# Mixing stage of a hybrid mLSTM and attention layer: gates ahead of the convolutions, splits in halves, reciprocal roots in nine steps, values of two head groups in 512 columns

## The chip, the cores and the metric

The kernel runs on one core of a Trainium2 chip. The metric is the time of one execution on the device in microseconds (us). PE is TensorE (matrix products), with PEld its weight loads, DVE is VectorE, ACT is ScalarE, POOL is GpSimd and SP is SyncE, which issues the DMAs. Each engine works through its own list of instructions in order, and waits at an instruction until its inputs are there and its output buffer is free.

## The reference

One layer acts on 512 tokens of 1024 columns, in float32. A conditioning vector `c` gives nine vectors of shift, scale and gate (`mod`). Then:

```python
u = rms_norm(x, ffn1_norm_g) * (1 + sc1) + sh1
x = x + 0.5 * g1 * swiglu(u, ffn1_w_in, ffn1_w_out)          # FFN1

u = rms_norm(x, mix_norm_g) * (1 + sc2) + sh2
z = u @ w_mix + b_mix                                        # mixing
q_m, k_m, v_m, o_m, i_m, f_m, q_f, k_f, v_f, f_f, g_a, g_b = split(z)
qk_m = silu(causal_conv([q_m, k_m], conv_w, conv_b))         # width 4
h_m = mlstm_chunkwise(q_m, k_m, v_m, i_m, f_m)               # 4 heads, 128 / 256
y_a = sigmoid(o_m) * rms_norm(h_m, mlstm_norm_g)
y_b = forgetting_attention(q_f, k_f, v_f, f_f, ...)          # 16 heads of 64
merged = sigmoid(g_a) * (y_a @ w_branch_a) + sigmoid(g_b) * (y_b @ w_branch_b)
x = x + g2 * (merged @ w_out)

u = rms_norm(x, ffn2_norm_g) * (1 + sc3) + sh3
x = x + 0.5 * g3 * swiglu(u, ffn2_w_in, ffn2_w_out)          # FFN2
```

`rms_norm` divides each row by the root of its mean square plus 1e-6. The gates of both mixers (i_m, f_m with 4 columns each, f_f with 16) go through log-sigmoid and cumulative sums over the tokens.

## The kernel before, in words

**Products.** Every float32 product is made of three products of shorter floats: each operand is split into a high part (`wh`, `uh`) and the rest (`wl`, `ul`), and `mm3` (L124 to L128) adds high by high (L126), high by low (L127) and low by high (L128) into one PSUM bank; which of the two operands is called weight or input depends on the caller. Which operand is held and which streams differs: a product streams 128 to 512 columns. A weight tile comes by DMA into a buffer `raw` (three of them, L91), ACT copies it to `wh` (L101) and DVE subtracts to get `wl` (L103); of `wh` and of `wl` there are four buffers each. Such a tile holds 1024 columns in each of 128 partitions, the gates' first two 840. PSUM has four banks named `g` and four named `t`.

**Order.** A scheduler orders the instructions of each engine from the order in which the program makes them and from the buffers; in some places the program pins its own order (`self.pin`), among them the function `end` (from L1315), which passes from FFN1 to the mixing stage.

**Roots.** `rsqrt` (L136 to L154) is made of DVE instructions on few columns: two for the first guess from the bits of the number, eight for a polynomial that corrects it. `xnorm` (L241) makes the mean square of two token blocks in two steps, calls `rsqrt`, and multiplies x (L253 on DVE, and a half on ACT) to `xn`; `chain` at the start of the kernel does the same. `mlstm_h` (each head) and `fox_qkv` (each group of four heads) call `rsqrt` as well, on 4 and 32 columns.

**From FFN1 to the mixing stage.** The 512 tokens are normalised in two halves. `xn` is transposed on PE (L295), and `u_part` (L270 to L280) makes `uh` and `ul` from it for each of eight blocks k of 128 columns. In `end`, the residual updates of x (`onto`, L600) and the squares of x for the second half (`x_sq`, L228) are interleaved with the first half's u parts and with the splits of the first four weight tiles of `w_mix`, m = 0 to 3 (`hi` makes `wh` and returns the subtraction for `wl`, L1328). `first(0)` and `first(1)` (L1380 to L1390) run the products of these four tiles with the first and with the second half of the tokens: lines L1387, L1388 and L1390, six products of 256 columns for each k and pair of m. Both halves go over k = 0 to 3 for m = 0, 1, then for m = 2, 3, then k = 4 to 7 the same way. Between `first(0)` and `first(1)` stand the second half's root, transposes and u parts.

**Then** (L1416 to L1425) come the convolutions of m = 0 to 3 (`qk_conv`: `cz` on ACT L917, four steps of `cy` on DVE L919 and L921, silu and high part on ACT, low part on DVE L926), then `gates` (L850), then m = 4 to 7 with a product and a convolution each. `gates` streams 280 columns: 256 columns of v_f (the values of head group 0, kept in DRAM as `v0` for later) and the gates' 24. Their weights come in three tiles (3, 3 and 2 blocks k), each of four DMA pieces. The results fill the four `t` banks; DVE adds biases (L861 and L862 into `gz`, L863 for v0), PE transposes `gz` (L880), and ACT and DVE make logs and scans. `columns()` runs after m = 7.

**Attention.** For each group g of four heads, `fox_qkv` (L1039) makes the queries and keys in one product of 512 columns (biases added into `tk`, L1047), the root over their squares (`rsqrt`), and then, for g = 1 to 3, the values in a product of 256 columns (two weight tiles of 4 blocks k). `donev` adds the bias (`vg`, L1073), ACT takes the high part and DVE the low part (L1078) into a tile `vm`, of which three exist. The call for group g + 1 is used as filling between the heads of group g, in pieces, followed by tiles of the merging gates (`with_gates(..., n)`).

Of the kernel before, what the change touches and what calls it, by code (L numbers as in the profile page):

```python
# [20 lines left out]
P = 128  # L21
# [9 lines left out]
RSQ = (0.2740822732448578, 0.31394892930984497, 0.37500056624412537, 0.4999983012676239, 1.0)  # L31
# [15 lines left out]
class Layer:  # L47
# [88 lines left out]
    def rsqrt(self, v, n, pin=lambda i: i):  # L136

        nc, sp = self.nc, self.sp
        y = sp.tile([P, n], F32, name=self.nm("rq"), tag=f"rq{n}", bufs=4)
        t = sp.tile([P, n], F32, name=self.nm("rt"), tag=f"rt{n}", bufs=2)  # L140
        d = sp.tile([P, n], F32, name=self.nm("rd"), tag=f"rd{n}", bufs=2)
        V = nc.vector
        pin(V.tensor_scalar(y.bitcast(I32), v.bitcast(I32), 1, None, op0=ALU.logical_shift_right))
        pin(V.tensor_scalar(y.bitcast(I32), y.bitcast(I32), -1, 0x5F3759DF, op0=MUL, op1=ADD))

        pin(V.tensor_tensor(t, y, y, op=MUL))
        pin(V.tensor_tensor(t, t, v, op=MUL))
# [5 lines left out]
        pin(V.scalar_tensor_tensor(y, t, RSQ[4], y, op0=ADD, op1=MUL))  # L153
        return y  # L154
# [86 lines left out]
    def xnorm(self, hf, pool):  # L241

        nc, sp = self.nc, self.sp
        v = sp.tile([P, 2], F32, name=self.nm("v"), tag="v", bufs=2)
        s2 = self.ss[:, 2 * hf:2 * hf + 2, :]
        self.pin(nc.vector.tensor_scalar(v, s2[:, :, 0], 1.0 / D, EPS, op0=MUL, op1=ADD))
        self.pin(nc.vector.scalar_tensor_tensor(v, s2[:, :, 1], 1.0 / D, v, op0=MUL, op1=ADD))
        r = self.rsqrt(v, 2, self.pin)
        xn = []
        for i in range(2):  # L250
            x = self.x[2 * hf + i]
            d = self.xn_tiles(pool)
            self.pin(nc.vector.tensor_scalar(d[0], x[0], r[:, i:i + 1], None, op0=MUL))  # L253
# [439 lines left out]
    def start(self, st, tp):  # L693
# [16 lines left out]
        def chain(hf):  # L710
            v = sp.tile([P, 2], F32, name=self.nm("v"), tag="v", bufs=2)
            s2 = self.ss[:, 2 * hf:2 * hf + 2, :]
            pin(nc.vector.tensor_scalar(v, s2[:, :, 0], 1.0 / D, EPS, op0=MUL, op1=ADD))
            pin(nc.vector.scalar_tensor_tensor(v, s2[:, :, 1], 1.0 / D, v, op0=MUL, op1=ADD))
            return self.rsqrt(v, 2, pin)
# [323 lines left out]
    def fox_qkv(self, g, ip):  # L1039
# [28 lines left out]
        bv = self.bias_bcast([(VF + o, 256)], ip) if g else None  # L1068
        vt = ip.tile([P, NT, 4, P], F32R, name=self.nm("fvt"), tag="vm", bufs=3)
        def donev(tb, ps):  # L1070
            f = ip.tile([P, 256], F32, name=self.nm("vg"), tag="t2", bufs=3)
# [5 lines left out]
            nc.scalar.activation(vt[:, tb, :, 0:64], f4, AF.Copy)  # L1077
            nc.vector.tensor_tensor(vt[:, tb, :, 64:P], f4, vt[:, tb, :, 0:64], op=SUB)  # L1078
        def mkv(ch):
            def make():  # L1080
                sh = [P, 4, 256]
                r = self.raw(sh, [(lambda t: t, w[ch * 512:(ch + 1) * 512, VF + o:VF + o + 256]
                                   .rearrange("(k p) n -> p k n", p=P))])
                wh, wl = self.split(r, sh)
                return wh, wl, 4 * ch, 4
            return make
        self.fx[g] = (tok, vt)
# [186 lines left out]
    def run(self):  # L1274
# [10 lines left out]
        with tc.tile_pool(name="f1t", bufs=1) as tp:  # L1285
# [5 lines left out]
            with tc.tile_pool(name="f1h", bufs=1) as hp:  # L1291
# [23 lines left out]
                def end(close, scaled, onto):  # L1315
# [110 lines left out]
        with tc.tile_pool(name="att", bufs=1) as ip:  # L1426
# [152 lines left out]
```

## Time and profile before

| | us |
|---|---|
| time, median of 3 runs (lowest to highest) | 1333.39 (1333.33 to 1336.34) |
| the profiled execution: its own time | 1333.93 |
| the profiled execution: span of the trace | 1332.2 |
| DVE `wl` by L103, 250 instructions: busy, one | 293.4, 1.175 |
| ACT `wh` by L101, 250 instructions: busy, one | 253.8, 1.018 |

The profile shows one execution. A row of the timeline gives the start and the duration in us, the engine, the line of the kernel, the operation, the output and the inputs, their size, how many equal instructions follow each other (`x4`: the duration is then from the first one's start to the last one's end), and in brackets how long the engine was idle before it and what ended that. In a row of waits stand the waiting engine, tile and line, then the engine, tile and line waited for, then the sum in us, the number and the longest. In a row of groups stand the count, the busy time, the mean of one in ns, and the idle time before. Products on PE overlap: the time from one start to the next is shorter than the duration of one.

### The profile page before, as it was taken

How to read it: one execution, taken by the hardware profiler on the slowest of the kernel's cores; microseconds unless marked ns; L12 is line 12 of the kernel's file. 1: busy time of each engine (PE TensorE's matmuls, PEld its weight loads, DVE VectorE, ACT ScalarE, POOL GpSimd, SP SyncE). 2: the span in 40 equal slices, each digit the busy share in tenths (PEclk: the TensorE clock that was granted, in tenths of full speed). 3: DMA queues.
4: the chain of work that ended last, by engine and by line, in shares of the span. 5: the costliest groups of instructions: out<-in, count | busy, mean ns of one | idle time of the engine just before them, and what ended most of it. 6: DMA issues, size and time to landing. Idle time of an engine off the chain costs nothing.

```text
span 1332.2 us, 18008 instructions
## 1 busy us (share of the span) xinstructions
PE 1311.0 (98%) x6428; PEld 1098.2 (82%) x6428; DVE 966.3 (73%) x1776; ACT 625.0 (47%) x1038; POOL 42.4 (3%) x65
## 2 busy tenths in 40 slices
PE   7999999999999999999999999999999999999998
PEld 6788888878788888888888788778788888888886
DVE  7877777477788687887877778777477656635777
ACT  5533323365476655566666666334253223223742
POOL 1000000000010101000000000003010000000000
PEclk9999999999999999999999999999999999999999
DMA  9999978365835334534252636777529877534574
GB/s 291 276 321 312 317 269 284 113 182 182 280 112 144 108 101 133 159 101 117 65 155 52 181 97 190 217 248 234 163 71 334 282 248 265 201 105 134 172 267 149
DMA packets 205514, 254.21 MB, mean 191 GB/s; under 512 B 15008, under 2 KB 148800, under 8 KB 205424
## 3 DMA queue, kind: packets, MB, share of 16 engines
q1 hardware_dynamic: 205040, 252.98, 60.6%
q8 instruction: 51, 0.84, 0.3%
q14 instruction: 39, 0.32, 0.1%
q0 software_dynamic: 320, 0.06, 0.0%
q10 hardware_dynamic: 64, 0.02, 0.0%
HBM read 217.28 MB, written 35.72 MB: 190 GB/s over the span
## 4 chain that ended last, share of the span: by engine, by line
PE 85%; DVE 7%; DMA 3%; ACT 3%; issue 1%; POOL 0%; ACTq 0%; SPq 0%; DVEq 0%; POOLq 0%
PE g L128 22%; PE g L127 22%; PE g L126 22%; PE t L127 3%; PE t L128 3%; PE t L126 3%; PE g L826 2%; DVE wl L103 2%; PE t L1200 1%; PE t L1170 1%; DMA raw<-in_ffn_w_out_dram 1%; ACT wh L101 1%; PE t L1141 1%; PE t L826 1%; PE t L1142 1%
## 5 line engine op out<-in xcount | busy, mean ns | idle before, releaser
L101 ACT ACTIVATE wh<-raw 128x1024 fp32r<-128x1024 f32 (+2 forms) x250 | 253.8, 1018 | 379.2 <-PE g L127 115.0
L103 DVE TENSOR_TENSOR wl<-raw,wh 128x1024 fp32r<-128x1024 f32 (+2 forms) x250 | 293.4, 1175 | 186.9 <-ACT wh L101 155.6
L127 PE MATMUL g<-ul,wh 128*128 128x512 f32 (+1 forms) x912 | 348.1, 383 | 0.6 <-DVE ul L267 0.3
L126 PE MATMUL g<-uh,wh 128*128 128x512 f32 (+1 forms) x912 | 348.2, 384 | 0.2 <-ACT wh L101 0.2
L128 PE MATMUL g<-uh,wl 128*128 128x512 f32 (+1 forms) x912 | 347.8, 382 | 0.0
L127 PEld LDWEIGHTS g<-ul,wh 128*128 128x128 f32 x912 | 171.3, 188 | 34.0 <-POOL ul L267 1.1
L128 PEld LDWEIGHTS g<-uh,wl 128*128 128x128 f32 x912 | 171.3, 188 | 33.3
L126 PEld LDWEIGHTS g<-uh,wh 128*128 128x128 f32 x912 | 170.8, 188 | 33.0 <-issue 0.6
L126 PE MATMUL g<-wh,uh 128*128 128x512 f32 (+1 forms) x288 | 103.0, 358 | 0.0
L128 PE MATMUL g<-wh,ul 128*128 128x512 f32 (+1 forms) x288 | 102.2, 355 | 0.0
L127 PE MATMUL g<-wl,uh 128*128 128x512 f32 (+1 forms) x288 | 102.0, 354 | 0.0
L325 DVE SCALAR_TENSOR_TENSOR acc<-raw,ccol,acc 128x512 f32<-128x512 f32 (+1 forms) x70 | 66.7, 973 | 30.6 <-DMA raw<-in_w_ada_dram 30.4
L127 PE MATMUL t<-wl,A 128*128 128x512 f32 x176 | 69.2, 393 | 1.1 <-DVE wl L103 1.1
L126 PE MATMUL t<-wh,A 128*128 128x512 f32 x176 | 69.3, 394 | 0.0
L126 PEld LDWEIGHTS g<-wh,uh 128*128 128x128 f32 x288 | 54.3, 189 | 7.7 <-DVE tk L1047 0.5
L128 PEld LDWEIGHTS g<-wh,ul 128*128 128x128 f32 x288 | 54.3, 188 | 7.6
L127 PEld LDWEIGHTS g<-wl,uh 128*128 128x128 f32 x288 | 54.3, 189 | 7.3
L128 PE MATMUL g<-yh,wl 128*128 128x512 f32 x128 | 50.5, 394 | 1.3 <-DVE wl L103 1.3
L127 PE MATMUL g<-yl,wh 128*128 128x512 f32 x128 | 50.2, 393 | 0.0
L126 PE MATMUL g<-yh,wh 128*128 128x512 f32 x128 | 49.9, 390 | 0.0
L455 ACT ACTIVATE A<-E 128x768 fp32r<-128x768 f32 x22 | 18.6, 846 | 55.1 <-DVE E L454 51.0
L1152 ACT ACTIVATE S<-S,mn 128x128 f32<-128x128 f32 (+1 forms) x64 | 35.6, 557 | 17.9 <-DVE mn L1144 9.3
(347 smaller groups left out, 2192.3 us busy)
## 6 DMA issues: line engine op xcount, KB each, us to landing
raw<-in_ffn_w_in_dram SPq DMA_DIRECT2D x82, 512.0 KB
raw<-in_w_ada_dram SPq DMA_DIRECT2D x56, 512.0 KB
raw<-in_w_mix_dram SPq DMA_DIRECT2D x46, 512.0 KB
sa<-in_ffn_w_out_dram SPq DMA_DIRECT2D x22, 512.0 KB
sb<-in_ffn_w_out_dram SPq DMA_DIRECT2D x44, 256.0 KB
ws<-sa SPq DMA_DIRECT2D x22, 512.0 KB
ws<-sb SPq DMA_DIRECT2D x44, 256.0 KB
raw<-ws SPq DMA_DIRECT2D x44, 256.0 KB
```

The lines of the kernel that those rows point to most:

```text
L101: nc.scalar.activation(hi, src, AF.Copy)
L103: self.last_lo = nc.vector.tensor_tensor(lo, src, hi, op=SUB)
L126: pin(mm(ps, lh, rh, start=start, stop=False))
L127: pin(mm(ps, lh, rl, start=False, stop=False))
L128: self.last_mm = pin(mm(ps, ll, rh, start=False, stop=stop))
L325: nc.vector.scalar_tensor_tensor(a, r[:, s], c, a, op0=MUL, op1=ADD)
L455: nc.scalar.activation(A1[:, 0:3, :], E[:, 0:3, :], AF.Copy)
L826: pin(nc.tensor.matmul(acc_ps[b], (wl if p == 1 else wh)[:, b % 2, s], self.ul[k] if p == 2 else self.uh[k], start=k == 0 and p == 0, stop ...
L1141: nc.tensor.matmul(ps[:, :w], q[:, s], k[:, :w], start=True, stop=False)
L1142: nc.tensor.matmul(ps[:, :w], q[:, s], kl[:, :w], start=False, stop=True)
L1152: nc.scalar.activation(S[:, ws], S[:, ws], AF.Exp, scale=-1.0, bias=m, accum_out=sm[:, qb:qb + 1])
L1170: tr = lambda b, c, qb, kb: nc.tensor.transpose(b[:, c:c + P], S[:, P_OFF[qb] + kb * P:P_OFF[qb] + (kb + 1) * P], self.ident)
```

## The change

- `run`: `gates()` is called before `qk_conv` of m = 0 to 3 instead of behind them.
- `end`: the `wl` subtractions of m = 2 and 3 (`lo2`, `lo3`) are done in halves (blocks 0 to 3 and 4 to 7) at later places; `onto(2, 0, ...)` moves behind the u parts 6 and 7. `first(1)` goes over all eight k for m = 0, 1 and then for m = 2, 3.
- `rsqrt` has eight DVE instructions instead of ten (one for the first guess, seven for a polynomial in two quadratic factors), and the mean square in `xnorm` and `chain` one instead of two.
- `fox_qkv`: the call for group 2 makes the values of groups 2 and 3 in one product of 512 columns (four weight tiles of two blocks k), the call for group 3 makes none. The numbers of gate tiles behind the calls go from 2, 4, 4 to 2, 2, 6.

In the built program this takes 96 matmuls of 6400 from PE, 36 instructions of 1778 from DVE and one DMA from SP; ACT and POOL keep their number.

```diff
-    def rsqrt(self, v, n, pin=lambda i: i):
+    def rsqrt(self, v, n, pin=lambda i: i, gain=1.0):
...
-        t = sp.tile([P, n], F32, name=self.nm("rt"), tag=f"rt{n}", bufs=2)
+        t, q = [sp.tile([P, n], F32, name=self.nm("rt"), tag=f"rt{n}", bufs=2) for _ in range(2)]
...
-        pin(V.tensor_scalar(y.bitcast(I32), v.bitcast(I32), 1, None, op0=ALU.logical_shift_right))
-        pin(V.tensor_scalar(y.bitcast(I32), y.bitcast(I32), -1, 0x5F3759DF, op0=MUL, op1=ADD))
+        s = (gain * RSQ_LEAD) ** 0.25
+        (a0, b0), (a1, b1) = [(a * s, b * s * s) for a, b in RSQ_QUADS]
+        pin(V.tensor_scalar(y.bitcast(I32), v.bitcast(I32), -0.5, 0x5F3759DF, op0=MUL, op1=ADD))
         pin(V.tensor_tensor(t, y, y, op=MUL))
-        pin(V.tensor_tensor(t, t, v, op=MUL))
-        pin(V.tensor_scalar(d, t, -1.0, 1.0, op0=MUL, op1=ADD))
-        pin(V.tensor_scalar(t, d, RSQ[0], RSQ[1], op0=MUL, op1=ADD))
-        pin(V.tensor_tensor(t, t, d, op=MUL))
-        pin(V.scalar_tensor_tensor(t, t, RSQ[2], d, op0=ADD, op1=MUL))
-        pin(V.scalar_tensor_tensor(t, t, RSQ[3], d, op0=ADD, op1=MUL))
-        pin(V.scalar_tensor_tensor(y, t, RSQ[4], y, op0=ADD, op1=MUL))
+        pin(V.scalar_tensor_tensor(d, t, -s, v, op0=MUL, op1=MUL))
+        pin(V.tensor_scalar(d, d, s, None, op0=ADD))
+        pin(V.scalar_tensor_tensor(t, d, a0, d, op0=ADD, op1=MUL))
+        pin(V.scalar_tensor_tensor(q, d, a1, d, op0=ADD, op1=MUL))
+        pin(V.scalar_tensor_tensor(y, t, b0, y, op0=ADD, op1=MUL))
+        pin(V.scalar_tensor_tensor(y, q, b1, y, op0=ADD, op1=MUL))
...
@@ xnorm, and the same in chain
-        self.pin(nc.vector.tensor_scalar(v, s2[:, :, 0], 1.0 / D, EPS, op0=MUL, op1=ADD))
-        self.pin(nc.vector.scalar_tensor_tensor(v, s2[:, :, 1], 1.0 / D, v, op0=MUL, op1=ADD))
-        r = self.rsqrt(v, 2, self.pin)
+        self.pin(nc.vector.scalar_tensor_tensor(v, s2[:, :, 0], D * EPS, s2[:, :, 1], op0=ADD, op1=ADD))
+        r = self.rsqrt(v, 2, self.pin, D ** 0.5)
...
@@ fox_qkv
+        if g == 3:
+            self.fx[g] = tok, self.fx[g]
+            return
+        gs = ((0,), (1,), (2, 3))[g]
+        n = len(gs) * 256
...
-                nc.vector.tensor_tensor(f, ps[:, :256], bv[:, :256], op=ADD)
+                nc.vector.tensor_tensor(f, ps[:, :n], bv[:, :n], op=ADD)
...
-            f4 = f.rearrange("p (h d) -> p h d", h=4)
-            nc.scalar.activation(vt[:, tb, :, 0:64], f4, AF.Copy)
-            nc.vector.tensor_tensor(vt[:, tb, :, 64:P], f4, vt[:, tb, :, 0:64], op=SUB)
+            for i, vt in enumerate(vts):
+                f4 = f[:, i * 256:(i + 1) * 256].rearrange("p (h d) -> p h d", h=4)
+                nc.scalar.activation(vt[:, tb, :, 0:64], f4, AF.Copy)
+                nc.vector.tensor_tensor(vt[:, tb, :, 64:P], f4, vt[:, tb, :, 0:64], op=SUB)
...
-                sh = [P, 4, 256]
+                k = 8 // (2 * len(gs))
+                sh = [P, k, n]
...
-            yield from self.u_gemm_tokens([mkv(c) for c in range(2)], 256, donev)
+            yield from self.u_gemm_tokens([mkv(c) for c in range(2 * len(gs))], n, donev)
...
@@ end
                     part(2, 3)
-                    lo2()
                     u[2]()
                     u[3]()
+                    lo2(0, 4)
                     w1 = scaled(W[1], 0)
-                    lo3()
+                    lo3(0, 4)
                     part(4, 5)
                     u[4]()
                     u[5]()
                     onto(2, 1, tx[0, 1])
-                    onto(2, 0, tx[0, 0])
+                    lo2(4, NK)
+                    lo3(4, NK)
                     part(6, 7)
                     u[6]()
                     u[7]()
+                    onto(2, 0, tx[0, 0])
...
-                        for ks in (range(4), range(4, NK)):
+                        for ks in ((range(NK),) if h else (range(4), range(4, NK))):
                             for ms in ((0, 1), (2, 3)):
...
@@ run
+            columns = self.gates(mp, yp)
             for m in range(4):
                 self.qk_conv(m, self.pp[m], yp, mp)
-            columns = self.gates(mp, yp)
...
-                    fill = with_gates(self.fox_qkv(g + 1, ip), 4 if g else 2) if g < 3 else (s for m in range(NK) for s in self.y_a(m, yp, ip))
+                    fill = with_gates(self.fox_qkv(g + 1, ip), (2, 2, 6)[g]) if g < 3 else (s for m in range(NK) for s in self.y_a(m, yp, ip))
```

More of the change, by code (lines that the diff above doesn't have):

```diff
@@ L30 @@
 BIG = 1e30
-RSQ = (0.2740822732448578, 0.31394892930984497, 0.37500056624412537, 0.4999983012676239, 1.0)
+RSQ_LEAD = 0.2740822732448578
+RSQ_QUADS = ((-1.0965162378196741, 1.8032570710297795), (2.2419713071789813, 2.0233052502305482))
 QM, KM, VM, OM, IG, FG, QF, KF, VF, FFG, GA, GB = (
@@ L1067, in fox_qkv @@
             nc.vector.tensor_tensor(t3, t3, r[:, tb * 8:(tb + 1) * 8].unsqueeze(2).to_broadcast([P, 8, 64]), op=MUL)
-        bv = self.bias_bcast([(VF + o, 256)], ip) if g else None
-        vt = ip.tile([P, NT, 4, P], F32R, name=self.nm("fvt"), tag="vm", bufs=3)
+        if g == 3:
[3 more added lines that the diff above has]
+        n = len(gs) * 256
+        bv = self.bias_bcast([(VF + o, n)], ip) if g else None
+        vts = [ip.tile([P, NT, 4, P], F32R, name=self.nm("fvt"), tag="vm", bufs=3) for _ in gs]
@@ L1070, in donev @@
         def donev(tb, ps):
-            f = ip.tile([P, 256], F32, name=self.nm("vg"), tag="t2", bufs=3)
+            f = ip.tile([P, n], F32, name=self.nm("vg"), tag="t2", bufs=3)
             if g:
-                nc.vector.tensor_tensor(f, ps[:, :256], bv[:, :256], op=ADD)
+                nc.vector.tensor_tensor(f, ps[:, :n], bv[:, :n], op=ADD)
             else:
                 nc.sync.dma_start(f, self.v0_d[tb])
-            f4 = f.rearrange("p (h d) -> p h d", h=4)
-            nc.scalar.activation(vt[:, tb, :, 0:64], f4, AF.Copy)
@@ L1083, in make @@
                                    .rearrange("(k p) n -> p k n", p=P))])
                 wh, wl = self.split(r, sh)
-                return wh, wl, 4 * ch, 4
+                return wh, wl, k * ch, k
             return make
-        self.fx[g] = (tok, vt)
+        self.fx[g] = (tok, vts[0])
+        if len(gs) > 1:
+            self.fx[3] = vts[1]
         if g:
-            yield from self.u_gemm_tokens([mkv(c) for c in range(2)], 256, donev)
+            yield from self.u_gemm_tokens([mkv(c) for c in range(2 * len(gs))], n, donev)
```

7 lines of the change are left out of this document (3 added, 4 removed).

## The prediction

> **What bounds the kernel now.** I read the page's head and chain first, then the busy time of each engine in five stretches, then what PE waits for around the edit, and then the time rows there.
>
> ```profile
> span 1332.2 us, 18008 instructions
> PE 1311.0 (98%) x6428; PEld 1098.2 (82%) x6428; DVE 966.3 (73%) x1776; ACT 625.0 (47%) x1038; POOL 42.4 (3%) x65
> ...
> PE 85%; DVE 7%; DMA 3%; ACT 3%; issue 1%; POOL 0%; ACTq 0%; SPq 0%; DVEq 0%; POOLq 0%
> ```
>
> PE (the matrix engine) is busy for 98% of the span, and 85% of the chain that ends last lies on it. So an edit counts only by what it takes off PE's own list, or by a gap of PE that it closes or opens. Work removed from DVE (73%) or ACT is worth nothing by itself.
>
> ```profile
> 60.00:270.00 210.00, 210.00 (x927) 173.11 (x926) 149.40 (x192) 67.39 (x77) 0.00 (x0) 1.00 0.82 272
> 375.00:425.00 50.00, 46.15 (x344) 43.76 (x343) 41.31 (x83) 33.10 (x61) 5.62 (x12) 1.00 0.41 105
> ...
> 560.00:770.00 210.00, 208.74 (x1186) 180.21 (x1184) 163.97 (x437) 131.13 (x269) 0.00 (x0) 1.00 0.39 112
> 950.00:1000.00 50.00, 49.01 (x301) 42.35 (x301) 32.98 (x72) 23.69 (x44) 5.95 (x8) 1.00 0.32 98
> ```
>
> The columns are the stretch, its length, then PE, PEld, DVE, ACT and POOL busy, the granted clock, the DMA share and GB/s. PE has no gap in the long weight stages (210.00 of 210.00), and the clock is 1.00 everywhere, so no term below comes from the clock. In the transition from FFN1 to the mixing stage (375 to 425 us) PE is idle for 3.85 us; in the attention stage for 1.26 us of 210; at the start of FFN2 for 0.99 us of 50. These three are the places where this edit can win time. PE's waits in the first of them:
>
> ```profile
> PE t L127 <- DVE wl L103: 2.8, 1, 2.8
> PE t L295 <- DVE xn L253: 0.7, 1, 0.7
> PE g L1388 <- DVE wl L1328: 0.2, 1, 0.2
> ```
>
> **The change part by part.**
>
> *1. Gates ahead of the convolutions (transition).* The 2.8 us wait is the gates' own product, waiting for the low half of its first weight tile:
>
> ```profile
> 404.82 0.68 PE L126 MATMUL t<-wh,uh 128*128 128x280 f32 x4
> 408.26 0.40 PE L127 MATMUL t<-wl,uh 128*128 128x280 f32 x1 [2.76 <-DVE wl L103]
> ...
> 420.41 0.48 PE L126 MATMUL g<-uh,wh 128*128 128x512 f32 x1
> ```
> ```profile
> 402.82 0.55 DVE L919 TENSOR_SCALAR cy<-cz,colA 128x512 f32<-128x512 f32 x1 [4.15 <-ACT cz L917]
> 404.53 2.73 DVE L921 SCALAR_TENSOR_TENSOR cy<-cz,colA,cy 128x512 f32<-128x512 f32 x4
> 407.18 1.02 DVE L103 TENSOR_TENSOR wl<-raw,wh 128x840 fp32r<-128x840 f32 x1
> ...
> 420.09 0.16 DVE L861 TENSOR_TENSOR gz<-t,bb 128x8 f32<-128x8 f32 x1
> 420.63 2.35 DVE L103 TENSOR_TENSOR wl<-raw,wh 128x1024 fp32r<-128x1024 f32 x2
> ```
> ```profile
> 402.02 1.27 ACT L917 ACTIVATE cz<-g,colA 128x512 f32<-128x512 f32 x2 [4.66 <-PE g L1390]
> 403.18 2.40 ACT L101 ACTIVATE wh<-raw 128x840 fp32r<-128x840 f32 x3
> ...
> 412.48 1.07 ACT L101 ACTIVATE wh<-raw 128x1024 fp32r<-128x1024 f32 x1 [1.86 <-DMA raw<-in_w_mix_dram]
> ```
>
> The bracket is the idle time of the engine and what ended it: DVE stood idle for 4.15 us and ACT for 4.66 us. Then ACT took two convolutions' inputs before the gates' wh, and DVE took two convolutions' steps (402.82 to about 407.2) before the gates' wl. PE ran the four high products that need no wl, 0.13 us apart, so the next was due at 404.82 + 4 x 0.13 = 405.34; it began at 408.26. **2.9 us** are lost. Why were the engines idle instead of splitting? All four wh and wl buffers held the weights of m = 0 to 3 until the second half's products were done. Now first(1) does m = 0, 1 over all eight k and then m = 2, 3, so two pairs of buffers come free halfway. Where that is comes out of these rows:
>
> ```profile
> 387.87 0.17 DVE L246 TENSOR_SCALAR v<-ss 128x2 f32<-128x2 f32 x1 [0.79 <-ACT rs L228]
> 390.06 0.16 DVE L153 SCALAR_TENSOR_TENSOR rq<-rt,rq 128x2 f32<-128x2 f32 x1
> 390.26 0.88 DVE L253 TENSOR_SCALAR xn<-x,rq 128x512 f32<-128x512 f32 x2
> ```
> ```profile
> 390.89 2.16 PE L295 MATMUL t<-ident,xn 128*128 128x128 f32 x16 [0.72 <-DVE xn L253]
> 392.81 0.36 PE L1387 MATMUL g<-uh,wh 128*128 128x256 f32 x1
> ```
> ```profile
> 642.50 0.28 PE L127 MATMUL g<-wl,uh 128*128 128x256 f32 x1
> ...
> 645.02 0.28 PE L127 MATMUL g<-wl,uh 128*128 128x256 f32 x1
> ...
> 571.00 0.39 PE L126 MATMUL g<-wh,uh 128*128 128x512 f32 x1
> ...
> 575.08 0.39 PE L126 MATMUL g<-wh,uh 128*128 128x512 f32 x1
> ```
>
> A product of 256 columns follows the one before by 0.120 us (642.50 to 645.02 is 21 of them), so 8 k x 6 products take 5.8 us: from 392.81 to 398.6, the last result at about 399.0, and 398.2 with the 0.8 us of part 2. ACT, free by then, needs 2.40/3 = 0.8 us for the first wh (399.0) and DVE 1.0 us for its wl (400.0). PE wants that wl at 404.5, so the 2.9 us go with 4 us to spare.
>
> What is late next? The transposes of gz stand right behind the gates' last product on PE, and wait for DVE's gz adds. Before, DVE ran from 402.82 to the third of these adds (420.09) in 17.3 us without a break; in the new order the stretch from the first gate split to that add loses one low half and one conv step (0.7 each) and gets one more split (2.35/2): about 17.1 us, so from 399.0 to 416.1. PE comes there at 404.5 + (420.27 - 408.26) = 416.5 (it was at the first two of those transposes at 420.27). The slack is 0.4 us in a list of 17; I book a loss of 0.1 (0 to 0.5).
>
> ```profile
> 387.54 1.81 SPq L934 DMA_DIRECT2D bb<-in_b_mix_dram  x4
> ...
> 389.39 29.66 SPq L91 DMA_DIRECT2D raw<-in_w_mix_dram  x8
> ```
>
> Queues: on SP the gates' bias pieces are issued at 387.5 to 389.3 and the last of their weight pieces right behind, ten microseconds ahead of their split; the change lets them stay there. The raw buffer of m = 4 comes free with the first gate split: before, that was 408.2, and its wh began at 412.48, 4.3 us later; now about 400 and 404.3, and it is wanted after the gates (416.5). GpSimd only gets the memsets of cz later. The convolutions, now behind the gates, are read after m = 7 alone. Term: -2.9 + 0.1 = **-2.8 us** (-2.9 to -2.3).
>
> *2. Split in halves, nine steps instead of twelve (transition).* The second half's root, from 387.87 to 390.06 and 0.16 more (ended by xn at 390.26), is 12 steps of 0.2 us (2.39/12); it becomes 9: 0.6 us earlier, and the transposes behind it (390.89) with it, since PE waits there (0.72). The x updates ahead of it end perhaps 0.2 us earlier, since u parts no longer stand behind a split of 1024 columns. I take -0.8 (-0.4 to -1.2). The wait for L1388 (0.2) goes as well, but only lengthens the wait for xn behind it: nothing. Term: **-0.8 us**.
>
> *3. Values of two groups in 512 columns.* 192 products of 256 columns become 96 of 512:
>
> ```profile
> L126 PE MATMUL g<-wh,uh 128*128 128x256 f32 x96 | 27.6, 288 | 0.0
> ```
>
> These 96 of L126, with as many of L127 and L128, are the three groups' values; two groups' share is 192. A product of 512 columns takes 4.08/18 = 0.2267 us (571.00 to 575.08), two of 256 take 0.240. 96 x 0.0133 = **-1.3 us**. The busy mean of 288 ns is no price here, since products overlap; the spacing is. The Trainium skill's page "TensorE: Matmul & The Clock Gate", section "Back-to-back issue gap", puts the spacing of an isolated product at N/2.4 + 2.5 ns. By that a pair saves 2.5 ns, an estimate of 0.24 us for 96, and the total would come out 1.0 us higher; the trace's spacing at 256 columns is 120 ns where the formula gives 109, so the trace has a larger fixed part, and I go by the trace.
>
> *4. Attention stage, other effects.* The stage has 1.26 us of gaps in all. Roots of eight steps instead of ten shorten a latency there, and the gate tiles that fill PE's list are dealt out differently (2, 2, 6 instead of 2, 4, 4).
>
> ```profile
> L1047 DVE TENSOR_TENSOR tk<-g,bb 128x512 f32<-128x512 f32 x16 | 10.4, 684 | 9.7 <-PE t L1113 9.6
> ...
> L1078 DVE TENSOR_TENSOR fvt<-vg,fvt 128x256 fp32r<-128x256 f32 x16 | 6.5, 414 | 0.3 <-ACT fvt L1077 0.3
> ```
>
> A finished bank of 512 value columns now costs DVE 0.68 + 2 x 0.41 = 1.5 us, so 6.0 us for four banks in one burst; what follows on PE needs the first of them at once but the second only after a gate tile of 24 products, 24 x 0.2267 = 5.4 us. If DVE has other work in between it costs the difference and a little more, 0.8 us; if nearly all gaps closed it would give 1.0. I take **-0.2 us** (+0.8 to -1.0). The same root stands once in the mLSTM heads where PE waits:
>
> ```profile
> 545.35 0.35 PE L126 MATMUL t<-vm,Wh 128*128 128x258 f32 x1 [0.48 <-DVE hn L1027]
> ```
>
> Two steps of 0.2 fewer ahead of it: **-0.3 us** (0 to -0.5).
>
> *5. Start of FFN2.* The same xnorm stands there, and PE has gaps of 0.99 us:
>
> ```profile
> 970.52 0.68 PE L295 MATMUL t<-ident,xn 128*128 128x128 f32 x4
> ...
> 991.58 0.38 PE L127 MATMUL g<-ul,wh 128*128 128x256 f32 x1 [0.31 <-DVE ul L267]
> ```
>
> With 0.6 us less of root, the transposes move ahead of products that cover the steps behind them. I take two thirds of the gaps: **-0.7 us** (0 to -1.0).
>
> *6. Start of the kernel.* The roots get shorter there too, but PE waits for ACT:
>
> ```profile
> 16.73 1.19 PE L826 MATMUL g<-uh,wh 128*128 128x512 f32 x4 [1.19 <-ACT uh L773]
> ```
>
> ACT's columns uh come out of the modulation as well as out of the root, and I count the root as hidden behind the modulation: **0** (+0.2 to -0.4, a third of that wait).
>
> Sum: -2.8 - 0.8 - 1.3 - 0.2 - 0.3 - 0.7 = **-6.1 us**. The profiled execution took 1333.93 us (its span 1332.2 and 1.7 around it), 0.54 above the median 1333.39. 1333.39 - 6.1 = **1327.3 us**.
>
> **The rivals.**
>
> *A, the forecast:* 1327.3 us.
>
> *B, the wait moves to the gates' gz adds.* The wl wait goes, but DVE's 17.1 us ahead of the gz transposes then set the end: a first gate split that starts d later than 399.4 costs d. With a start at 400.9, as if ACT had two u parts of the second half and a tile of wh still in front of it, 1.5 us are lost there, and with the 0.8 of part 2 gone as well (DVE late in its whole list) the time is 1327.3 + 1.5 + 0.8 = **1329.6 us**. For it: the slack is 0.4 us, and DVE is busy for 41.31 of these 50 us. Against it: DVE had 4.15 us of idle time just there.
>
> *C, slower: the buffers do not come free halfway.* A split waits for the last reader of the buffer that it takes over. If the gates' splits start only when all of first(1) is done (404.0), wh is there at 404.8 and wl at 405.8, which holds PE for 1.3 us; the gz adds then end at 404.8 + 17.1 = 421.9 and PE arrives at 405.8 + 12.0 = 417.8, held 4.1 us more. 5.4 us are lost instead of 2.9 + 0.8: the stage is 1.7 us longer than before. The point from which it decides is a first gate split at 399.4 + 3.7 = 403.1. With the small terms at nothing and the values' 1.3 it gives 1333.39 + 1.7 - 1.3 = **1333.8 us**, slower than before; with the attention burst's 0.8, 1334.6. For it: the trace of before shows all of these buffers freed together, at the end. Against it: the new order frees m = 0 and 1, the oldest two, first.
>
> *D, the values' merge gives only what the page's formula gives* (part 3): 1327.3 + 1.0 = **1328.3 us**. The trace's 120 ns against 109 speaks against that rule. It lies inside A's own ends.
>
> **How the numbers follow.** A 0.75 with D in it, B 0.16, C 0.06, and 0.03 for a cost that I did not see. A's own ends: all gains at their upper bounds, -2.9 - 1.2 - 1.3 - 1.0 - 0.5 - 1.0 - 0.4 = -8.3 (1325.1); terms 4 to 6 missing and half of part 2, -4.5 (1328.9). The range reaches over B to **1324.8 to 1330.8**. A measurement of this kernel can tell 0.3% (4.0 us) from no change: faster means below 1329.4. A's lower part and a third of B fall there: **faster 0.77, same 0.19, slower 0.04**. (C at 1334 is within 0.3%; only with more late splits does it pass 1337.4.)
>
> **What would show it.** In the changed kernel's trace: the wait of the first L127 with 280 columns gone, its wl split starting at about 399 to 400 and before the first convolution step; the transposes of gz without a wait over 0.5 us; xn's transposes at about 390.1 instead of 390.89; the group of 256 columns of `wh,uh` down from 96 to 32 and the 512s up by 32 on each line, spacing 0.227; FFN2's gaps (950 to 1000) below 0.6 us. It would be wrong if the first gate split started after 403, if a new wait on gz over 1 us appeared, or if the attention stage's PE gaps grew beyond 2 us.

## The result, and the profile after

The changed kernel takes 1328.04 us (median of 5 runs, 1325.84 to 1328.99), the kernel before 1334.26 (median of 5, 1333.33 to 1336.34): a ratio of 0.9949 with a 95% interval of 0.9935 to 0.9963, so 6.8 us less by the ratio. A repeat on another chip gave 0.9948 (0.9934 to 0.9962). One execution of a later kernel (the one that makes a subtraction four times over) ran in a slower state, at 1868.43 us and a mean clock of 0.655, and is left out of its median and count. The profiled execution took 1328.68 us, its span 1326.9. Lines of `split`, `mm3` and what follows stand one or two numbers later than before (`wl` L103 is L104, the three products L126 to L128 are L127 to L129).

The page's head and chain, then the busy time in two of the stretches shown of before:

```profile
span 1326.9 us, 17767 instructions
PE 1308.3 (99%) x6332; PEld 1091.9 (82%) x6332; DVE 959.9 (72%) x1740; ACT 622.6 (47%) x1038; POOL 43.8 (3%) x65
...
PE 91%; DVE 4%; ACT 2%; DMA 2%; issue 1%; POOL 0%; SPq 0%; ACTq 0%; DVEq 0%; POOLq 0%
```
```profile
375.00:425.00 50.00, 49.43 (x366) 46.86 (x364) 42.22 (x85) 34.84 (x64) 5.90 (x13) 1.00 0.46 122
560.00:770.00 210.00, 208.79 (x1096) 175.29 (x1095) 167.03 (x435) 132.04 (x275) 0.00 (x0) 1.00 0.38 111
```

PE's idle time in the transition fell from 3.85 to 0.57 us; in the attention stage it is where it was (1.21 against 1.26). Of PE's waits between 370 and 425 us one row is left:

```profile
PE t L295 <- DVE xn L253: 0.4, 1, 0.4
```

The time rows of the transition, PE, then DVE, then ACT:

```profile
391.67 2.17 PE L295 MATMUL t<-ident,xn 128*128 128x128 f32 x16 [0.36 <-DVE xn L253]
...
405.60 0.29 PE L127 MATMUL t<-wh,uh 128*128 128x280 f32 x1
405.73 0.29 PE L128 MATMUL t<-wl,uh 128*128 128x280 f32 x1
...
418.09 0.77 PE L879 MATMUL t<-ident,gz 128*96 128x128 f32 x3
418.62 0.48 PE L127 MATMUL g<-uh,wh 128*128 128x512 f32 x1
```
```profile
400.86 1.98 DVE L104 TENSOR_TENSOR wl<-raw,wh 128x840 fp32r<-128x840 f32 x2 [1.48 <-ACT wh L102]
402.75 1.00 DVE L918 TENSOR_SCALAR cy<-cz,colA 128x512 f32<-128x512 f32 x2
...
418.26 0.15 DVE L860 TENSOR_TENSOR gz<-t,bb 128x8 f32<-128x8 f32 x1
```
```profile
399.92 1.70 ACT L102 ACTIVATE wh<-raw 128x840 fp32r<-128x840 f32 x2 [1.79 <-PE g L1400]
401.53 1.25 ACT L916 ACTIVATE cz<-g,colA 128x512 f32<-128x512 f32 x2
```

The gates' products with wh and with wl now follow each other 0.13 us apart: the 2.8 us wait is gone. Both low halves run at 400.86, ahead of the first convolution step, four microseconds before PE asks. Three transposes of gz span 0.77 us from 418.09; in the run with the gates moved alone, below, three take 0.49. 0.24 us is lost on the third gz add (418.26), 17.4 us behind the start of the wl; 17.1 were forecast. The two traces' times can't be compared one by one (PE's first instruction comes at 6.27 us instead of 4.81), but the wl starts 9.2 us behind xn's transposes; 8.9 were forecast (390.1 to 399.0).

The share of time in which PE is busy hides short delays, since products overlap. So for the terms I added up, over all neighbours on PE, the time from start to start less the usual spacing of that size (0.227 us for 512 columns, 0.129 for 280, 0.120 for 256, 0.109 for the transposes). The lost time by stretch of the two profiled executions:

| stretch, us | before | after | difference | predicted |
|---|---|---|---|---|
| 0 to 67 | 7.7 | 7.4 | -0.3 | 0 |
| 67 to 366, FFN1 | 3.3 | 4.0 | +0.7 | 0 |
| 366 to 400, roots and halves | 2.35 | 1.31 | -1.0 | -0.8 |
| 400 to 433, gates | 3.10 | 0.43 | -2.7 | -2.8 |
| 433 to 560, with the mLSTM | 1.0 | 0.9 | -0.1 | -0.3 |
| 560 to 770, attention | 5.66 | 5.67 | 0 | -0.2 |
| 770 to 933, branches | 3.4 | 1.5 | -1.9 | 0 |
| 933 to 1000, FFN2's start | 4.13 | 3.65 | -0.5 | -0.7 |
| from 1000 | 0.9 | 1.2 | +0.3 | 0 |
| the products themselves | | | -1.2 | -1.3 |

The sum is -6.7 us, against 6.77 on PE from its first to its last instruction. Two of these rows (FFN1 and the branches) are not the change's: see the end of the experiments.

### The profile page after: what moved, and what is told of

It is laid out like the page before. It is cut to its first block, busy times and chain, and to the rows that moved or that the text cites. A ratio compares the mean times of both kernels' runs of the same rounds, so it can differ in the third digit from the quotient of the medians.

```text
span 1326.9 us, 17767 instructions
## 1 busy us (share of the span) xinstructions
PE 1308.3 (99%) x6332; PEld 1091.9 (82%) x6332; DVE 959.9 (72%) x1740; ACT 622.6 (47%) x1038; POOL 43.8 (3%) x65
## 4 chain that ended last, share of the span: by engine, by line
PE 91%; DVE 4%; ACT 2%; DMA 2%; issue 1%; POOL 0%; SPq 0%; ACTq 0%; DVEq 0%; POOLq 0%
PE g L127 23%; PE g L129 23%; PE g L128 23%; PE t L128 4%; PE t L127 4%; PE t L129 4%; PE g L825 2%; PE t L1208 1%; PE t L1178 1%; DMA x<-x_d 1%; DVE wl L104 1%; PE t L1149 1%; PE t L825 1%; PE t L1150 1%; ACT wh L102 0%
## 5 line engine op out<-in xcount | busy, mean ns | idle before, releaser
L104 DVE TENSOR_TENSOR wl<-raw,wh 128x1024 fp32r<-128x1024 f32 (+2 forms) x250 | 292.9, 1174 | 178.0 <-ACT wh L102 154.8
L128 PE MATMUL g<-ul,wh 128*128 128x512 f32 (+1 forms) x912 | 348.1, 383 | 1.0 <-POOL ul L267 1.0
L127 PE MATMUL g<-uh,wh 128*128 128x512 f32 (+1 forms) x912 | 348.5, 384 | 0.0
L129 PE MATMUL g<-uh,wl 128*128 128x512 f32 (+1 forms) x912 | 348.2, 382 | 0.0
L128 PEld LDWEIGHTS g<-ul,wh 128*128 128x128 f32 x912 | 171.3, 188 | 34.3 <-POOL ul L267 1.8
L129 PEld LDWEIGHTS g<-uh,wl 128*128 128x128 f32 x912 | 171.4, 188 | 33.2
L127 PEld LDWEIGHTS g<-uh,wh 128*128 128x128 f32 x912 | 171.0, 188 | 32.8 <-issue 0.6
L127 PE MATMUL g<-wh,uh 128*128 128x512 f32 (+1 forms) x256 | 97.4, 380 | 0.0
L129 PE MATMUL g<-wh,ul 128*128 128x512 f32 (+1 forms) x256 | 96.6, 377 | 0.0
L128 PE MATMUL g<-wl,uh 128*128 128x512 f32 (+1 forms) x256 | 96.4, 377 | 0.0
L128 PE MATMUL t<-wl,A 128*128 128x512 f32 x176 | 69.3, 394 | 1.7 <-DVE wl L104 1.6
L127 PE MATMUL t<-wh,A 128*128 128x512 f32 x176 | 69.3, 394 | 0.1
L129 PEld LDWEIGHTS g<-wh,ul 128*128 128x128 f32 x256 | 48.2, 188 | 9.0
L127 PEld LDWEIGHTS g<-wh,uh 128*128 128x128 f32 x256 | 48.2, 188 | 8.7 <-DVE tk L1046 0.5
L128 PEld LDWEIGHTS g<-wl,uh 128*128 128x128 f32 x256 | 48.2, 188 | 8.3
L127 PE MATMUL g<-yh,wh 128*128 128x512 f32 x128 | 50.4, 394 | 0.0
L129 PE MATMUL g<-yh,wl 128*128 128x512 f32 x128 | 50.2, 392 | 0.0
L128 PE MATMUL g<-yl,wh 128*128 128x512 f32 x128 | 49.7, 388 | 0.0
```

Of the source, the lines that this page charges most:

```text
L104: self.last_lo = nc.vector.tensor_tensor(lo, src, hi, op=SUB)
L127: pin(mm(ps, lh, rh, start=start, stop=False))
L128: pin(mm(ps, lh, rl, start=False, stop=False))
L129: self.last_mm = pin(mm(ps, ll, rh, start=False, stop=stop))
```

## The experiments

**What closes the gates' wait.** Four kernels move gates() and turn first(1) separately. Theory H, from the prediction: what counts is that the weight buffers come free halfway. Rival O: the order alone is enough.

*Gates alone*, on the kernel before:

```diff
+            columns = self.gates(mp, yp)
             for m in range(4):
                 self.qk_conv(m, self.pp[m], yp, mp)
-            columns = self.gates(mp, yp)
```

> The kernel before with one edit: gates() stands ahead of the four convolutions; first(1) keeps its old order of k, so the four pairs of weight buffers come free only when first(1) is done. Theory H (halfway release decides): ACT's first 840-column wh starts at 404.9 as its reader's release allows, DVE's wl ends at about 406.7, PE still waits for it 1.0 to 1.6 us (2.76 before), and the gz transposes then wait 1.5 to 4 us behind DVE; the stage from 375 to 425 us gains nothing, time within -0.5 to +1.7 us of before. Rival O (the order of the program alone decides): the wl wait is below 0.5 us, no wait at gz over 0.5, time 2.5 to 3 us below before.

Measured: ratio 0.9978 (0.9968 to 0.9987), about 2.9 us less. ACT and PE in its trace:

```profile
402.65 1.70 ACT L101 ACTIVATE wh<-raw 128x840 fp32r<-128x840 f32 x2 [4.65 <-PE g L1390]
```
```profile
405.45 0.29 PE L126 MATMUL t<-wh,uh 128*128 128x280 f32 x1
405.58 0.29 PE L127 MATMUL t<-wl,uh 128*128 128x280 f32 x1
...
417.94 0.49 PE L880 MATMUL t<-ident,gz 128*96 128x128 f32 x3
```

There is no wait for wl and none at gz; 0.31 us is lost at 445 us instead, where PE waits for ACT's `cz`. Theory H fell. ACT's wh starts at 402.65, 2.8 us ahead of the end of first(1), on a release by L1390. The reason lies in the old order itself: k = 0 to 3 for m = 0, 1, then for m = 2, 3, then k = 4 to 7 for m = 0, 1, and only then for m = 2, 3. So m = 0 and 1 are done after three quarters. The row of ACT's `cz` in the prediction (402.02, ended by L1390, while PE's gate products begin at 404.82) showed just that, and was read as the end of everything. DVE's list ahead of the third gz add took 13.9 us here (403.59 to 417.45), not 17.1: the scheduler put the adds ahead of convolution steps, so that 7 of those on L921 stood before the third add and not 11 as in the changed kernel. With a list of 17.1 us from 403.59 that add would have come at 420.7, an estimate, 2.5 us after the start of PE's third transpose (418.16).

*Gates and first(1)*, on the kernel before, is the run above and this:

```diff
-                        for ks in (range(4), range(4, NK)):
+                        for ks in ((range(NK),) if h else (range(4), range(4, NK))):
```

> The kernel before with two edits: gates() ahead of the convolutions, and first(1) over all eight k for m = 0, 1 and then m = 2, 3. Roots, splits and values as before. Theory H: ACT's first 840-column wh starts near 399.3, DVE's first wl near 400.1, PE's wait for wl is gone, the gz transposes wait below 0.5 us; xn's transposes still at about 390.9; 2.5 to 3.0 us below before, about 1331.4 if before is 1334.3. Rival B (the wait moves to the gz adds): a new wait of 1.5 us or more at the gz transposes, and 1 us or less gained. Rival O: the same time as the run with gates() moved alone.

Measured: ratio 0.9971 (0.9962 to 0.9980), about 3.9 us less; its interval overlaps with that of gates alone. The wl wait is gone, and 0.38 us is lost at the gz transposes. The halfway release adds nothing that these runs can tell.

*The changed kernel with the old first(1)* undoes that line:

```diff
-                        for ks in ((range(NK),) if h else (range(4), range(4, NK))):
+                        for ks in (range(4), range(4, NK)):
```

> The changed kernel with first(1) back in its old order of k (0 to 3 for both pairs of m, then 4 to 7); all other edits stay. Theory H: PE waits again for the gates' first wl, 1.0 to 1.6 us, and 1.5 to 4 us at gz: 2.5 to 4.5 us above the changed kernel, so 1.5 to 4 us below before. Rival O: no wait there, the same time as the changed kernel, 6 us below before.

Measured: ratio 0.9944 (0.9932 to 0.9956), no wait at wl or at gz; 0.33 us is lost at 444 us instead. The turned first(1) is worth nothing once the gates stand ahead: O held.

*The changed kernel with the gates back behind the convolutions*, but first(1) turned:

```diff
-            columns = self.gates(mp, yp)
             for m in range(4):
                 self.qk_conv(m, self.pp[m], yp, mp)
+            columns = self.gates(mp, yp)
```

> The changed kernel with gates() back behind the four convolutions; first(1) keeps its new order, so buffers come free halfway. If the release alone decides, the gates' wh runs on ACT near 400 all the same and PE's wait for wl is below 0.5 us: the time of the changed kernel. If both edits are needed (theory H in full: DVE's list still has convolution steps ahead of the wl), PE's wait for wl is 0.5 to 2.5 us, and the time is 1 to 3 us above the changed kernel.

Measured: ratio 0.9952 (0.9940 to 0.9964). PE and DVE:

```profile
404.57 0.42 PE L127 MATMUL t<-wh,uh 128*128 128x280 f32 x2
405.13 0.40 PE L128 MATMUL t<-wl,uh 128*128 128x280 f32 x1
```
```profile
404.05 1.03 DVE L104 TENSOR_TENSOR wl<-raw,wh 128x840 fp32r<-128x840 f32 x1
```

The wl comes at 405.08, and PE loses 0.30 us. So either edit without the other takes 2.6 to 2.9 us of the 2.9 of this wait away; they are two cures of one wait, and the second one made is worth 0 to 0.3 us. (The turned first(1) ran without the gates' move only in the changed kernel, beside its other edits.)

**Roots and halves.** Each alone on the kernel before.

```diff
-    def rsqrt(self, v, n, pin=lambda i: i):
+    def rsqrt(self, v, n, pin=lambda i: i, gain=1.0):
...
-        r = self.rsqrt(v, 2, self.pin)
+        r = self.rsqrt(v, 2, self.pin, D ** 0.5)
```

> The kernel before with only the nine-step roots (eight for the heads and groups). My terms 2, 4 and 5: xn's wait at the second half falls from 0.88 us over the spacing to 0.3, the mLSTM wait falls by 0.3, FFN2's gaps by 0.3 to 0.7: 0.9 to 1.6 us below before. Rival R1: each root's steps overlap with other waits (ACT's half of xn, the squares), so that the waits shrink by less than half of the steps: 0.2 to 0.6 us. The wait for wl at the branch product near 838 us stays.

```diff
-                    lo2()
                     u[2]()
                     u[3]()
+                    lo2(0, 4)
...
+                    lo2(4, NK)
+                    lo3(4, NK)
                     part(6, 7)
...
+                    onto(2, 0, tx[0, 0])
```

> The kernel before with only the wl subtractions of m = 2 and 3 in halves and onto(2, 0) behind the u parts. My term: the two waits in first(0) (0.24 and 0.32 us over the spacing) go, and xn's wait behind them grows by nearly as much, so the sum of the three falls by about 0.2 us. Rival S1: the waits go and xn comes earlier by as much, 0.5 us or more in sum. Time within 0.7 us of before either way; the three rows decide.

Measured: roots 0.9990 (0.9981 to 0.9999), halves 0.9988 (0.9979 to 0.9997): each about 1.3 to 1.6 us by the times, with an interval of 2.4 us. The traces tell more. Roots only, then halves only:

```profile
390.07 0.40 PE L1389 MATMUL g<-ul,wh 128*128 128x256 f32 x2
390.39 1.83 PE L295 MATMUL t<-ident,xn 128*128 128x128 f32 x13
```
```profile
389.27 0.40 PE L1392 MATMUL g<-ul,wh 128*128 128x256 f32 x2
390.84 1.40 PE L295 MATMUL t<-ident,xn 128*128 128x128 f32 x9 [1.18 <-DVE xn L253]
```

With the roots alone the wait for xn, 0.88 us over the spacing before, is gone, and the two small waits of first(0) stay (0.23 and 0.31). With the halves alone these two go (0.56 in sum) and the wait for xn grows to 1.34: a net gain of 0.1. That is what term 2 said of the first(0) waits. Both together leave 0.52, so in the change the stretch gains 1.0 us, 0.8 of it by the roots alone. The second half's root took 1.58 us (389.45 to 391.03 in the changed kernel) where it took 2.39: 0.8 less, not 0.6, for three steps fewer. The two factors of the new polynomial don't use each other's result, and the second starts 0.08 us behind the first, not 0.20:

```profile
390.44 0.16 DVE L151 SCALAR_TENSOR_TENSOR rt<-rd 128x2 f32<-128x2 f32 x1
390.52 0.15 DVE L152 SCALAR_TENSOR_TENSOR rt<-rd 128x2 f32<-128x2 f32 x1
390.64 0.16 DVE L153 SCALAR_TENSOR_TENSOR rq<-rt,rq 128x2 f32<-128x2 f32 x1
```

In FFN2 the roots take the wait of the transposes away, but the u parts then arrive late. The waits of the changed kernel between 960 and 1000 us, and the longest:

```profile
PE g L128 <- POOL ul L267: 1.0, 3, 0.5
```
```profile
986.66 0.39 PE L128 MATMUL g<-ul,wh 128*128 128x256 f32 x1 [0.54 <-POOL ul L267]
```

Transposes that move ahead hand PE's wait on to GpSimd's `ul`: 0.5 us won of the 0.7 forecast. PE's idle time between 950 and 1000 us did not fall (1.03 us after, 0.99 before); what was won lies in delays too short to leave PE idle. In the mLSTM heads the same happened on a smaller scale; what ends the wait is now `fq`, not `hn`:

```profile
543.16 0.36 PE L127 MATMUL t<-vm,Wh 128*128 128x258 f32 x1 [0.38 <-DVE fq L1128]
```

**Values.** Alone on the kernel before, and the reverse of it on the changed kernel:

```diff
+        gs = ((0,), (1,), (2, 3))[g]
...
-            yield from self.u_gemm_tokens([mkv(c) for c in range(2)], 256, donev)
+            yield from self.u_gemm_tokens([mkv(c) for c in range(2 * len(gs))], n, donev)
...
-with_gates(self.fox_qkv(g + 1, ip), 4 if g else 2)
+with_gates(self.fox_qkv(g + 1, ip), (2, 2, 6)[g])
```

> The kernel before with only the values of groups 2 and 3 in one product of 512 columns and the gate tiles dealt 2, 2, 6. My term: 96 products fewer, spacing 0.120 and 0.2267, so PE's list is 1.3 us shorter; nothing else moves in the attention stage (its gaps 1.1 to 1.5 us). Rival V1: by the spacing of N/2.4 + 2.5 ns only 0.24 us. Rival V2: the new deal of tiles also moves the weight loads behind the stage, and the 1.0 us wait for wl at the branch product (near 838 us before) goes: 2.3 us below before, with that row gone in this run and present in the two runs with only roots and only halves.

> The changed kernel with the values back in 256 columns per group and the gate tiles dealt 2, 4, 4. My term: 1.3 us above the changed kernel and the wait near 835 us at the branch product as in the changed kernel (none). V1: 0.24 us above. V2: 2.3 us above, with the branch wait of about 1.0 us back.

Measured: alone 0.9984 (0.9974 to 0.9995), about 2.1 us; the change without them 1329.52 us, 0.9950 (0.9937 to 0.9962), on the same chip; the changed kernel on other chips took 1328.04 and 1328.26, 1.3 to 1.5 less. By the ratios to the kernel before (0.9950 against 0.9949 and 0.9948), each taken on one chip, the merge is worth 0.1 to 0.3 us, with intervals of 1.7 to 1.9 us to either side: the times can't tell 1.3 us from 0.24, and the rows have to. The groups in the changed kernel, and the first and last rows of a stretch of 21 products of 512 columns:

```profile
L127 PE MATMUL g<-wh,uh 128*128 128x512 f32 x224 | 88.3, 394 | 0.0
L127 PE MATMUL g<-wh,uh 128*128 128x256 f32 x32 | 9.0, 282 | 0.0
```
```profile
659.28 0.40 PE L127 MATMUL g<-wh,uh 128*128 128x512 f32 x1
...
664.07 0.28 PE L1149 MATMUL t<-fk,fq 128*128 128x256 f32 x1
```

64 products of 256 columns became 32 of 512 on each line, at 4.79/21 = 0.228 us: 96 x (0.240 - 0.228) = 1.2 us. V1 (0.24 us) fell by the spacing. V2 fell too: the wait at the branch product near 838 us went in the run with the values only, but also in that with the halves only and in the change without the values. The stretch from 770 to 933 us lost anything from 1.5 to 4.3 us in the 14 traces at hand, 1.5 and 3.5 in two traces of the changed kernel itself. PE's waits there, in the kernel before and in the repeat of the changed kernel:

```profile
PE g L128 <- DVE wl L103: 1.3, 2, 0.9
```
```profile
PE g L129 <- DVE wl L104: 1.3, 1, 1.3
```

So the -1.9 of the table is mostly the luck of two executions, as the +0.7 in FFN1 is (one wait for a wl between 360 and 363 us, from nothing to 1.0 us in the traces). What sets their size from run to run stays open.

**The clock.** In the three traces that keep the gates' 2.9 us wait (roots, halves, values alone) the stretch from 400 to 433 us lost 4.6 to 5.9 us instead of 3.1. Windows of the kernel before, and of values alone; the third column from the end is the granted clock:

```profile
408.00:412.00 4.00, 3.74 (x29) 3.75 (x30) 4.00 (x7) 2.08 (x4) 0.10 (x1) 1.00 0.63 146
```
```profile
408.00:412.00 4.00, 3.08 (x14) 3.08 (x15) 4.00 (x6) 2.75 (x5) 0.10 (x1) 0.66 0.46 121
409.26:412.68 3.42, 3.42 (x17) 3.42 (x16) 3.42 (x6) 1.73 (x3) 0.10 (x1) 0.50 0.69 170
```

Behind the wait the clock was 0.66 in the mean of 4 us, with 14 products where the other execution had 29. Cut finer, it was 0.50 for 3.41 us, from 409.26 to 412.68; halves alone has the same, and roots alone 0.50 for twice as long (407.08 to 413.91). To see whether the gap does it, three kernels make a gap of a chosen length in the changed kernel: GpSimd makes the first wl, two, three or four times over.

```diff
-    def split(self, src, shape):
+    def split(self, src, shape, pool=0):
...
-            self.last_lo = nc.vector.tensor_tensor(lo, src, hi, op=SUB)
+            for eng in [nc.gpsimd] * pool or [nc.vector]:
+                self.last_lo = eng.tensor_tensor(lo, src, hi, op=SUB)
...
-                wh, wl = self.split(self.raw(sh, dmas), sh)
+                wh, wl = self.split(self.raw(sh, dmas), sh, 0 if k0 else 2)
```

> The changed kernel once more, for the same chip as the three runs beside it. Its time 6 to 7 us below before; mean granted clock 0.999 or 1.000 in nearly every execution, since no gap of PE over 1 us is left between 375 and 450 us.

> The changed kernel, but the low half of the gates' first weight tile is made by GpSimd, twice over into the same tile, instead of once by DVE. From the 512-column subtractions on GpSimd (1.3 to 2.1 us) an estimate of 2.1 to 3.4 us each: PE's gap ahead of its first 280-column product with wl is 0 to 1.9 us. Theory K (a gap of PE drops the granted clock for some us behind it, the likelier the longer it is): no drop or a rare one; time 0 to 2 us above the changed kernel. Rival L (the drops seen behind the 2.8 us wait come from that stage's work or from the chip, not from the gap): drops as often as in the kernel before.

> The same, three times over: a gap of 1.4 to 5.3 us. Theory K: the clock in the 4 us behind the gap is 0.5 to 0.7 in some or most executions, so the mean clock is 0.998 in many of them, and the time is above the changed kernel by the gap and up to 2.8 us more. The Trainium skill's page on TensorE and the clock gate, section on the clock gate's states, gives a free-running window of about 3.4 us; by it the chance of a drop would rise with the gap and be certain past two windows. Rival L: the time grows by the gap alone, clock 1.00.

> The same, four times over: a gap of 3.5 to 8.7 us. Theory K: a drop to 0.5 to 0.7 behind the gap in nearly every execution, mean clock 0.998 or 0.997, time above the changed kernel by the gap and 1.5 to 2.8 us more. Rival L: by the gap alone, clock 1.00.

Measured, with the number of timed executions at a mean clock of 0.998 or less:

| kernel | longest gap on PE from 375 to 450 us, us | time at a clock of 0.50 behind it, us | median, us | executions at 0.998 or less |
|---|---|---|---|---|
| changed, repeat | 0.5 | none | 1328.26 | 0 of 5 |
| twice | 2.7, at gz | 3.41 | 1331.79 | 4 of 8 |
| three times | 2.1 | 3.41 | 1332.42 | 4 of 10 |
| four times | 4.2 | 6.83 | 1333.98 | 8 of 10 |
| before, three chips | 2.9 | none in the profile | 1334.99 to 1335.25 | 36 of 72 |

The windows of four times, and its PE rows:

```profile
407.18:410.60 3.42, 1.43 (x6) 1.43 (x7) 3.42 (x4) 0.99 (x1) 1.94 (x1) 0.50 0.11 16
410.60:414.01 3.41, 3.41 (x17) 3.41 (x17) 3.41 (x6) 1.65 (x4) 0.20 (x2) 0.50 0.49 138
```
```profile
404.85 0.29 PE L128 MATMUL t<-wh,uh 128*128 128x280 f32 x1
409.17 0.60 PE L129 MATMUL t<-wl,uh 128*128 128x280 f32 x1 [4.04 <-POOL wl L105]
```

Theory K held and L fell: the drop follows the gap, also where the gap lies elsewhere (in twice over, at 419.49 us), and a mean of 0.998 or less comes in 36 of 72 executions of the kernel before, but in 1 of 50 of the six kernels without the wait (gates alone, gates and first(1), the changed kernel, and it without first(1), gates or values). The count is a lower bound of the drops: a clock of 0.50 for 3.41 us lowers the mean of 1332 us by 0.0013, and the end of the execution, where the clock falls once PE is done, by up to 0.0009 more in the 14 traces. So a mean of 0.999 can hide a drop (the profiled execution of three times does), and only 1.000, which 12 of the 72 have, rules it out: by these numbers between 36 and 60 of the 72 had one.

Why the same gap has it in one execution and not in the next can be read from the traces. Each change of the clock in a trace lies a whole number of steps of 3.413 us from the others. With each trace cut into these steps, from its first change of the clock to the last products, a drop begins behind every step in which PE stood idle for 1.93 us or more (six traces, 1.93 to 2.76, by the modelled ends of the products) and behind no other; the largest idle time of a step without a drop behind it is 1.52 us. The profiled execution of before has its gap cut in two, 1.24 and 1.52 us of idle time (the second column is the length, the third PE's busy time):

```profile
403.32:406.74 3.42, 2.18 (x18) 1.95 (x17) 3.38 (x7) 2.35 (x4) 0.00 (x0) 1.00 0.00 0
406.74:410.15 3.41, 1.89 (x14) 1.90 (x15) 3.41 (x5) 2.87 (x6) 0.20 (x2) 1.00 0.20 30
```

That is read off the 14 traces, not tested by a run of its own, and why roots alone stayed at 0.50 for a second step, with only 0.68 us of idle time in the first, is open. What a drop costs is less sure: 1.5 us for one step and 2.8 for two by the lost time of the traces, but the 36 executions of before at 0.998 or less have a median only 0.8 us above the 12 at 1.000. As an estimate, the closed gap takes 0.4 us (36/72 x 0.8) to 1.6 us (60/72 x 1.9, the mean of the three traces) more off on average than its length. The Trainium skill's page "TensorE: Matmul & The Clock Gate", section "What's actually happening", has the clock fall to half after an idle window of about 3.4 us, in windows that run freely. The halved clock agrees (0.50), so do the steps of 3.41 us, and so does that the same gap has it in one execution and not in another; but gaps of 2.1 and 2.7 us, shorter than that window, had it too: no run here needed a window that was idle throughout.

Twice over did not give the gap where it was expected: the wl came in time, and PE stood still ahead of the transposes of gz instead (2.7 us). DVE was slower while GpSimd worked, as told at the end, and made its first gz add 18.5 us behind its first subtraction (15.8 in the changed kernel).

No version tried is clearly better than the changed kernel: the one with the old first(1) took 1327.4 us on another chip, within the spread.

## Why the prediction was right

The forecast was 1327.3 us and -6.1 us; measured were 1328.04 and -6.2 by the medians (-6.8 by the ratio). By its steps:

- *Part 1, the gates (-2.8):* -2.7 in the trace. Right in size, wrong in the reason. The size is partly luck: whatever removes the wait wins its whole length and no more. The step that failed is "All four wh and wl buffers held the weights of m = 0 to 3 until the second half's products were done": two of them came free at three quarters, 2.8 us before the end, and moving the gates alone closes the wait, as does the turned first(1) without it in the changed kernel. The forecast slack of 0.4 us at gz was a loss of 0.24 (0.1 was booked).
- *Rival C* could not happen, for the same reason: gates alone is its mechanism, and gained 2.9 us; DVE's list up to the third gz add was also 13.9 us there and not C's 17.1. *Rival B* named the right next wait, and it cost 0.24 us, not 1.5.
- *"No term below comes from the clock"* failed. The profiled execution of before happened to be one without the drop; between 36 and 60 of 72 have it, and the closed gap takes an estimated 0.4 to 1.6 us more off on average. That can fill the difference between the terms that the change owns (-1.0 - 2.7 - 0.1 - 0.5 - 1.2 = -5.5) and the 6.8 of the ratio; but the interval of the ratio (4.9 to 8.7 us) holds 5.5 as well, so this isn't shown. It is luck that the sum comes so near: terms 0.6 us too large and a clock that was counted as nothing offset each other.
- *Part 2 (-0.8):* -1.0; the root became 0.8 us shorter, not 0.6; the roots were worth 0.8, the halves 0.1 to 0.3 alone and 0.2 on top.
- *Part 3 (-1.3):* 1.2 by count and spacing. *Rival D*, with 0.24, was wrong by the spacing; the times alone could not tell.
- *Part 4 (-0.2 and -0.3):* 0 and -0.1: shorter roots handed PE's waits to others. The burst of 512 value columns on DVE cost nothing. *Part 5 (-0.7):* -0.5, for the waits on GpSimd's `ul`; the sign that PE's gaps there fall below 0.6 us failed (1.03). *Part 6 (0):* 0.

## What to carry to other kernels

Before a wait is put down to a buffer, follow the order of its readers to the last one: here two of four buffers came free at three quarters, and the row that said so was on the page. A gap of 2 to 4 us on TensorE can cost more than its length, since the clock behind it may drop; whether it does depends on where the gap falls, and one profile can miss it, so compare the mean clock over many executions. Two edits that cure the same wait don't add up.

## What was not expected of the hardware

- The granted clock fell to 0.50 for 3.41 us, or for 6.83, behind gaps of 2.1 to 4.2 us on TensorE: behind the gap of 2.9 us in 36 to 60 of 72 executions, by their mean clock. It cost 1.5 to 2.8 us by the lost time of three traces, and 0.8 by the medians of the executions.
- DVE slowed down while GpSimd subtracted. With GpSimd at work from 400.15 to 409.12, DVE's own subtraction of 840 columns took 2.15 us (0.99 in the changed kernel, where two take 1.98), and two convolution steps that take 1.00 us took 4.33. Each of the three took about as long as one of GpSimd's four subtractions (8.97/4 = 2.24 us):

```profile
400.15 8.97 POOL L105 TENSOR_TENSOR wl<-raw,wh 128x840 fp32r<-128x840 f32 x4 [11.79 <-ACT wh L102]
```
```profile
400.90 2.15 DVE L105 TENSOR_TENSOR wl<-raw,wh 128x840 fp32r<-128x840 f32 x1 [2.28 <-ACT wh L102]
402.97 4.33 DVE L919 TENSOR_SCALAR cy<-cz,colA 128x512 f32<-128x512 f32 x2
```

The Trainium skill's page "GPSIMD Engine Reference", section "1. Specifications", says that GpSimd shares its SBUF interfaces with VectorE, and that this meets VectorE's instructions in a two-port mode or with two inputs from SBUF. The subtraction has two; the convolution's first step reads one tile, and slowed down the more. Whether it ran in a two-port mode, no run here shows.
